# One weight unit of the compression moved to the room of the transposed queries, and the on-chip tiles at other addresses

## The chip, the cores and the metric

The kernel runs on one core of a Trainium2 chip. The metric is the device time of one launch in microseconds (us). The kernel before took 658.87 us, the median of three runs (658.71 to 659.05).

## The reference

Two layers of a decoder trunk on 256 tokens of width 1024, in float32. Each layer normalises its input, projects it once, feeds three groups of heads, projects their joined output back, and runs an MLP.

```
for l in range(DEPTH):                                  # DEPTH = 2, 256 tokens, width 1024
    h = rms_norm(x, ln1_gain[l])
    proj = h @ w_in[l]                                  # 1024 x 2866, cut into q, k, v, gates, ...
    o_nsa = nsa_mixer(...)                              # compressed, selected and window branches, 6 heads
    o_mla = mla_mixer(...)                              # low-rank attention, 5 heads
    o_ret = retention_mixer(...)                        # chunkwise retention, 5 heads
    x = x + concatenate([o_nsa, o_mla, o_ret]) @ w_out[l]
    h = rms_norm(x, ln2_gain[l])
    x = x + jnp.square(jax.nn.relu(h @ w_up[l])) @ w_down[l]        # 1024 -> 4096 -> 1024
return rms_norm(x, final_gain)
```

The change touches the first step of the compressed branch. Blocks of 32 keys and of 32 values, one starting every 16 tokens, get a position embedding and go through a two-layer network of their own:

```
blk = tok[:, tok_idx] + pos_emb[None, None, :, None, :]     # 15 blocks of 32 tokens
flat = blk.transpose(...).reshape(b, 15, g, 32 * 64)
return jax.nn.gelu(flat @ w1) @ w2                          # w1: 2048 x 128, one for keys, one for values
```

## The kernel before

**Engines.** TensorE (PE) multiplies, VectorE (DVE), ScalarE (ACT) and GpSimd (POOL) do the elementwise work, SyncE (SP) issues nearly all transfers. Each engine works through its instructions in a fixed order, and waits where the next one is not ready. That order is made when the program is built: the kernel's lines are issued with priorities (the table `PRIO`, the calls of `prio`), and a scheduler with a model of the durations sets the order of each engine from them. So where a tile gets its room later or earlier, the scheduler may order every engine anew.

**Products.** Each float32 operand is cut into a high part and a low part, both in a rounded 32-bit type. `mm3` (L151 to L153) makes one product of three matmuls. In the in-projection, in the out-projection and in the down projection the weights are the moving operand (384, 320, 434 or 512 columns at a time) and the activations are loaded into the array as stationary tiles of 128 x 128. In the up projection it is the other way round: weights stationary, the transposed activations `xT` moving, 512 columns with `hi_wu` (L1120) and 256 with `lo_wu` (L1121). There are 512 such pairs (the first 32 of them under the name `l_pu`).

**Weights.** They stream in units of 4 KB a partition, in the order of a list that the class `Stream` walks: for each layer `A`, the low-rank weights, `B2`, the small tables of the compression, `B1` (4 units, queries), `w1` (4 units: two for keys, two for values), `B3` (4 units), `rq`, `rk`, `rg`, `rv`, `wo`, then `wu` and `wd` of the MLP. A unit is loaded to a raw tile (`raw_tile`, pool `rawp`, five buffers, DMAs at L328), cut by a cast on ACT (L145, high part) and a subtraction on DVE (L146, low part) into tiles of the pool `splitp` (five buffers each), and used from there. A raw buffer comes free when both have read it. The `w1` units (L421) are not cut: the matmuls of `ps_h` (L775) read the raw tiles, so four of the five raw buffers stay occupied from their load until `ps_h` has run, and the units behind them, `B3_0` to `B3_3` and `rq_0`, pass one after another through the fifth.

**The stretch around the compression.** ACT scales a value tile (`l_vm`, L669), copies transposed queries and keys (`l_qkT`, L677), copies the transposed blocks `l_T` (L756, L758, L760) and the key tile `l_kT`, and cuts units of `B3` in between. When both halves of `l_T` are there, PE runs the 64 small matmuls of `ps_h` (L775). ACT copies the result to `h_sb` (L778), PE transposes and folds it into `ps_hT` (L781), and behind it on PE come the matmuls of `B3`. The chain from `ps_hT` over a gelu to `kc_` gives the compressed keys that the scores need later.

**Where the tiles lie.** Pools are laid out in the order in which they are opened. In the built program of the kernel before, all large tiles (raw, high and low parts of weights, `xs`, the scratch tiles, `xT`, the mixer's output, the probabilities and `u_h`, `u_l` of the MLP) start at 128 modulo 1024 bytes of a partition. `xT` (16 KB) lies in the pool `whole`; so do the transposed queries `qT0` and `qT1` (3 KB each), which are written for the first time after `ps_h` and last read by the scores of the same layer.

Of the kernel before, what the change touches and what calls it, by code (L numbers as in the profile page):

```python
# [7 lines left out]
F32 = mybir.dt.float32  # L8
F32R = mybir.dt.float32r
# [5 lines left out]
P = 128  # L15
D = 1024
S = 256
# [10 lines left out]
C_ID, C_INV, N_C0 = 0, 128, 176  # L28
# [49 lines left out]
def tile_hybrid_trunk(  # L78
# [25 lines left out]
):  # L104
    nc = tc.nc

    rawp = ctx.enter_context(tc.tile_pool(name="rawp", bufs=RAW))
    splitp = ctx.enter_context(tc.tile_pool(name="splitp", bufs=SPL))
    whole = ctx.enter_context(tc.tile_pool(name="whole", bufs=1))
    const = ctx.enter_context(tc.tile_pool(name="const", bufs=1))  # L110
    p1 = ctx.enter_context(tc.tile_pool(name="p1", bufs=1))
    p2 = ctx.enter_context(tc.tile_pool(name="p2", bufs=2))
# [3 lines left out]
    def prio(key):  # L116

        return tc.high_priority(offset=PRIO[key]) if key in PRIO else nullcontext()
# [7 lines left out]
    def wk(name, chain="N"):  # L126

        return wkp.tile([P, 512], F32, name=name, tag="wk" + chain)

    def scr(name, shape, dtype=F32, chain="N"):  # L130

        if chain == "N":
            return whole.tile(shape, dtype, name=name, tag="sN", bufs=5)
        return p2.tile(shape, dtype, name=name, tag="sM", bufs=7)
# [8 lines left out]
    def split(hi, lo, src, eng=nc.vector):  # L143

        a = nc.scalar.copy(out=hi, in_=src)  # L145
        b = eng.tensor_tensor(lo, src, hi.bitcast(F32), op=ALU.subtract)  # L146
        return a, b
# [9 lines left out]


    xs = whole.tile([P, 2, D], F32, name="xs")
    c0s = const.tile([P, N_C0], F32, name="c0s")  # L160
    c1s = const.tile([P, N_C1], F32, name="c1s")
    pos_i = const.tile([P, 2], I32, name="pos_i")
    xv = x.rearrange("o (t p) d -> p (o t) d", p=P)
# [21 lines left out]

    nc.gpsimd.dma_start(pos_i, positions.rearrange("o (t p) -> p (o t)", p=P))
    ident = c0s[:, C_ID:C_ID + P]
    gT = const.tile([P, 8], F32, name="gT")
    tri = c1s[:, C_TRI:C_TRI + 384]
    valid = c1s[:, C_VALID:C_VALID + 1]  # L190
    blk = c1s[:, C_BLK:C_BLK + 384]
# [123 lines left out]
    def raw_tile(name):  # L315
        return rawp.tile([P, 1024], F32, name="raw_" + name, tag="raw")
# [43 lines left out]
    def add_side(l, name, f):  # L360
        def load():
            side[l, name] = f()
        W.add((l, name), load)
# [37 lines left out]

    def add_cmp(l):
        def small():
            w2s = p1.tile([P, 3, 64], F32, name=f"l{l}_w2s", tag="w2s")
            pos_t = p1.tile([P, 2, 2, 64], F32, name=f"l{l}_pos_t", tag="pos_t")
            for z, (pe, w2) in enumerate(((cmp_pos_k, cmp_w2_k), (cmp_pos_v, cmp_w2_v))):
                nc.sync.dma_start(w2s[:, 2 * z], w2[l])
                for rep in range(8):
                    nc.sync.dma_start(pos_t[rep * 16:(rep + 1) * 16, z], pe[l].rearrange("(b a) d -> a b d", b=2))
            nc.sync.dma_start(w2s[:, 1], cmp_w2_k[l])  # L410
            return w2s, pos_t

        add_side(l, "cmp", small)

    def add_w1(l):
        for z, w1 in enumerate((cmp_w1_k, cmp_w1_v)):
            for i in range(2):
                def load(z=z, w1=w1, i=i):
                    raw = raw_tile(f"w1_{l}{z}{i}")
                    for b in range(2):  # L420
                        nc.sync.dma_start(  # L421
                            raw[b * 64:(b + 1) * 64].rearrange("p (a h) -> p a h", a=8),
                            w1[l, b * 1024 + i * 512:b * 1024 + (i + 1) * 512].rearrange("(a d) h -> d a h", d=64))
                    return raw
                W.add((l, "w1", z, i), load)
# [53 lines left out]
            add_down(l, c)  # L479


    xT2 = whole.tile([P, 8, 2, S], F32R, name="xT", tag="xT")
    xT = [xT2[:, :, i] for i in range(2)]

    class Line:
# [70 lines left out]
    for l in range(DEPTH):  # L556
        L = f"l{l}_"
# [171 lines left out]
        w2s, pos_t = side[l, "cmp"]  # L729
# [46 lines left out]
        with prio("cmp"):  # L776
            hs_ = scr("h_sb", [P, 256])
            nc.scalar.copy(out=hs_, in_=psh[:, 0:256])  # L778
            pst = wk("ps_hT")
            for z in range(2):  # L780
                nc.tensor.matmul(pst[:, z * 32:(z + 1) * 32], hs_[:, z * P:(z + 1) * P], fold, start=True, stop=True)  # L781
            hT = p2.tile([P, 64], F32, name="hT", tag="hT", bufs=1)
            g1 = p2.tile([P, 64], F32, name="g1", tag="g1", bufs=1)
            g2 = p2.tile([P, 64], F32, name="g2", tag="g2", bufs=1)
            nc.vector.tensor_copy(out=hT, in_=pst[:, 0:64])

            nc.vector.tensor_tensor(g1, hT, hT, op=ALU.mult)
            nc.vector.tensor_scalar(g1, g1, 0.044715, 1.0, op0=ALU.mult, op1=ALU.add)
            nc.vector.tensor_tensor(g1, g1, hT, op=ALU.mult)
            nc.scalar.activation(g2, g1, AF.Tanh, scale=0.7978845608028654)  # L790
            nc.vector.scalar_tensor_tensor(g1, in0=g2, scalar=1.0, in1=hT, op0=ALU.add, op1=ALU.mult)
            gv = p2.tile([P, 2, 3, 16], F32, name="gv", tag="gv", bufs=1)
            nc.gpsimd.tensor_copy(gv, g1[:, 32:64].rearrange("p (g n) -> p g n", g=2).unsqueeze(2)
                                  .broadcast_to([P, 2, 3, 16]))
            pc = wk("ps_kc")
            nc.tensor.matmul(pc[:, 0:32], w2s[:, 0:2].rearrange("p b d -> p (b d)"), g1[:, 0:32], start=True, stop=True)
            nc.tensor.matmul(pc[0:96, 64:128], gv.rearrange("p g r n -> p (g r n)"), w2s[:, 2], start=True, stop=True)
            kc_ = p2.tile([P, 32], F32, name="kc_", tag="kc_", bufs=1)
            nc.scalar.mul(kc_, pc[:, 0:32], 0.5)
            split(kT[0][:, :, 256:272], kT[1][:, :, 256:272], kc_.rearrange("p (g n) -> p g n", g=2))  # L800
            vcb = p2.tile([96, 3, 2, 64], F32, name="vcb", tag="vcb", bufs=1)
            nc.vector.tensor_tensor(vcb, blk[0:96].rearrange("p (r g d) -> p r g d", r=3, g=2),
                                    pc[0:96, 64:128].unsqueeze(1).unsqueeze(1).broadcast_to([96, 3, 2, 64]),
                                    op=ALU.mult)

        qT = [whole.tile([P, 3, S], F32R, name=f"{L}qT{g}", tag=f"qT{g}") for g in range(2)]
        kv_sb = [None, None]

        def evac_b1(t, ps):
# [511 lines left out]
```

## Time and profile before

| what | value |
|---|---|
| median of three runs | 658.87 us (658.71 to 659.05) |
| profiled execution | 659.2 us, of which its span 657.4 us |
| granted TensorE clock, mean over the span | 0.990 of 2.4 GHz |
| PE busy | 639.2 us, 97% of the span |
| DVE, ACT, POOL busy | 459.1 us (70%), 380.5 us (58%), 68.0 us (10%) |
| transferred | 111.64 MB, mean 170 GB/s |

The span runs from the first instruction to the last. A row of a timeline has the start, the duration, the engine, the line, the operation, output and inputs, the shape and how many instructions are joined; in square brackets is how long the engine stood idle before it and what ended that. The matmul rows overlap, since matmuls are pipelined: what one costs in a run of equals is the distance from start to start, not the duration.

### The profile page before, as it was taken

To read this page: it belongs to the slowest core of one execution; us is meant where nothing else is said; L and a number is where in the kernel's file an instruction comes from. 1 tells how busy PE (TensorE), PEld (TensorE's weight loads), DVE (VectorE), ACT (ScalarE), POOL (GpSimd) and SP (SyncE) were. 2 spreads that over 40 slices of the span, in tenths; PEclk is the share of its full clock that TensorE was granted. 3 is DMA by queue.
4 is the path that set the end of the run, shared out by engine and by line. 5 is a ranking of instruction groups with operands and counts; after the bars stand their busy time and mean duration, and the time that the engine had idled before them with its cause. 6 is when DMAs were issued, how large, how long until landed. Compare 5 with 4: busy or idle time off the path is not lost.

```text
span 657.4 us, 10417 instructions
## 1 busy us (share of the span) xinstructions
PE 639.2 (97%) x3619; PEld 549.4 (84%) x3619; DVE 459.1 (70%) x1063; ACT 380.5 (58%) x895; POOL 68.0 (10%) x124
## 2 busy tenths in 40 slices
PE   5999999999999999999999999999999999999995
PEld 4998998677888888888889999967688888888884
DVE  6666988767756666666685698887695666666663
ACT  5768786555546444444476887836364645444442
POOL 3320500300000000000023132120100000000000
PEclk7899999999999999999999999999999999999999
DMA  7877637152756565655538574532376465646521
GB/s 242 260 164 232 202 102 200 36 157 72 253 191 218 167 207 178 194 191 188 162 113 208 178 222 130 146 97 82 107 263 191 163 219 162 219 164 218 167 65 64
DMA packets 79796, 111.64 MB, mean 170 GB/s; under 512 B 9720, under 2 KB 67968, under 8 KB 79616
## 3 DMA queue, kind: packets, MB, share of 16 engines
q1 hardware_dynamic: 79136, 108.89, 53.9%
q0 software_dynamic: 608, 2.10, 1.0%
q8 instruction: 28, 0.46, 0.3%
q14 instruction: 24, 0.20, 0.1%
HBM read 109.92 MB, written 1.05 MB: 169 GB/s over the span
## 4 chain that ended last, share of the span: by engine, by line
PE 91%; DVE 3%; ACT 2%; DMA 1%; issue 1%; SPq 1%; POOL 0%; POOLq 0%; ACTq 0%
PE ps_up L1120 17%; PE l_pd L151 9%; PE l_pd L152 9%; PE l_pd L153 9%; PE ps_up L1121 9%; PE l_B L152 2%; PE l_B L153 2%; PE l_B L151 2%; PE l_oT L908 2%; PE l_po L151 2%; PE l_po L153 2%; PE l_po L152 2%; PE ps_pT L916 1%; PE l_pu L1120 1%; PE l_A L151 1%; PE ps_sm L694 1%
## 5 line engine op out<-in xcount | busy, mean ns | idle before, releaser
L1120 PE MATMUL ps_up<-xT,hi_wu 128*128 128x512 f32 x480 | 170.0, 398 | 0.0
L1121 PE MATMUL ps_up<-xT,lo_wu 128*128 128x256 f32 x480 | 133.6, 280 | 0.0
L146 DVE TENSOR_TENSOR lo_wd<-raw_wd,hi_wd 128x1024 fp32r<-128x1024 f32 x64 | 78.2, 1224 | 50.8 <-ACT hi_wd L145 50.4
L1120 PEld LDWEIGHTS ps_up<-xT,hi_wu 128*128 128x128 f32 x480 | 89.8, 188 | 21.4
L152 PE MATMUL l_pd<-lo_wd,u_h 128*128 128x512 f32 x256 | 99.9, 390 | 0.0
L151 PE MATMUL l_pd<-hi_wd,u_l 128*128 128x512 f32 x256 | 99.8, 391 | 0.0
L153 PE MATMUL l_pd<-hi_wd,u_h 128*128 128x512 f32 x256 | 99.6, 389 | 0.0
L145 ACT CAST hi_wu<-raw_wu 128x512 fp32r<-128x512 f32 x128 | 72.9, 618 | 40.8 <-issue 26.9
L146 DVE TENSOR_TENSOR lo_wu<-raw_wu,hi_wu 128x512 fp32r<-128x512 f32 x128 | 82.4, 685 | 18.2 <-ACT hi_wu L145 18.0
L1121 PEld LDWEIGHTS ps_up<-xT,lo_wu 128*128 128x128 f32 x480 | 90.6, 189 | 1.6
L145 ACT CAST hi_wd<-raw_wd 128x1024 fp32r<-128x1024 f32 x64 | 67.1, 1051 | 30.9 <-PE l_pd L153 20.5
L151 PEld LDWEIGHTS l_pd<-hi_wd,u_l 128*128 128x128 f32 x256 | 48.1, 188 | 10.4
L153 PEld LDWEIGHTS l_pd<-hi_wd,u_h 128*128 128x128 f32 x256 | 48.1, 188 | 10.2
L152 PEld LDWEIGHTS l_pd<-lo_wd,u_h 128*128 128x128 f32 x256 | 48.1, 188 | 8.8
L145 ACT CAST u_h<-u_u 128x512 fp32r<-128x512 f32 x32 | 19.8, 620 | 48.9 <-DVE u_u L1136 48.8
L1133 ACT COPY u_s<-ps_up 128x256 f32<-128x256 f32 x60 | 22.1, 369 | 40.1 <-PE ps_up L1121 40.1
L146 DVE TENSOR_TENSOR lo_B<-raw_B,hi_B 128x192 fp32r<-128x192 f32 (+1 forms) x80 | 28.7, 414 | 20.9 <-ACT hi_B L145 20.9
L1134 DVE TENSOR_TENSOR u_s<-ps_up,u_s 128x256 f32<-128x256 f32 x60 | 25.1, 420 | 25.9 <-ACT u_s L1133 25.9
L872 ACT ACTIVATE p_nsa<-p_nsa,nsa_m 128x256 f32<-128x256 f32 (+2 forms) x72 | 28.4, 397 | 11.0 <-DVE nsa_m L870 11.0
L146 DVE TENSOR_TENSOR u_l<-u_u,u_h 128x512 fp32r<-128x512 f32 x32 | 22.1, 690 | 16.8 <-ACT u_h L145 16.6
L152 PE MATMUL l_B<-lo_B,xT 128*128 128x384 f32 x96 | 32.9, 342 | 0.2 <-DVE lo_B L146 0.2
L151 PE MATMUL l_B<-hi_B,xT 128*128 128x384 f32 x96 | 32.8, 348 | 0.0
(325 smaller groups left out, 1266.2 us busy)
## 6 DMA issues: line engine op xcount, KB each, us to landing
raw_wu<-in_w_up_dram SPq DMA_DIRECT2D x64, 512.0 KB, 4.5
raw_wd<-in_w_down_dram SPq DMA_DIRECT2D x64, 512.0 KB, 4.2
raw_B<-in_w_in_dram SPq DMA_DIRECT2D x24, 384.0 KB, 3.6
raw_wo<-in_w_out_dram SPq DMA_DIRECT2D x10, 512.0 KB, 3.5
raw_A<-in_w_in_dram SPq DMA_DIRECT2D x8, 434.0 KB, 4.5
raw_wo<-in_w_out_dram SPq DMA_DIRECT2D x12, 256.0 KB, 4.1
raw_w<-in_cmp_w_k_dram SPq DMA_DIRECT2D x8, 256.0 KB, 4.1
raw_w<-in_cmp_w_v_dram SPq DMA_DIRECT2D x8, 256.0 KB, 3.9
```

The lines of the kernel that those rows point to most:

```text
L145: a = nc.scalar.copy(out=hi, in_=src)
L146: b = eng.tensor_tensor(lo, src, hi.bitcast(F32), op=ALU.subtract)
L151: nc.tensor.matmul(o, a[1], b[0], start=start, stop=False)
L152: nc.tensor.matmul(o, a[0], b[1], start=False, stop=False)
L153: return nc.tensor.matmul(o, a[0], b[0], start=False, stop=stop)
L694: nc.tensor.matmul(ps[:, i * 256:i * 256 + nk], qkT[:, 5 + h, t * P:(t + 1) * P], qkT[:, h, 0:nk], start=True, stop=True)
L872: nc.scalar.activation(p[:, o:o + n], p[:, o:o + n], AF.Exp, scale=-1.0, bias=ms[:, r, b:b + 1], accum_out=ls[:, r, b:b + 1])
L908: nc.tensor.matmul(oT[gp, 0:384], kv_sb[kt][:, vi, gp], pTs[g][:, 0:384], start=i == 0, stop=False)
L1120: nc.tensor.matmul(ps[j], w[0][:, o:o + P], x2, start=i == 0 and k == 0, stop=False)
L1121: last = nc.tensor.matmul(ps[j][:, 0:S], w[1][:, o:o + P], x2[:, 0:S], start=False, stop=i == 1 and k == 3)
L1133: nc.scalar.copy(sj, ps[j][:, S:512])
L1134: nc.vector.tensor_tensor(sj, ps[j][:, 0:S], sj, op=ALU.add)
```

## The change

Two things change. First, of the four `w1` units of a layer the first (keys, first half) goes to a tile of the pool `whole` with the tag `qT`, whose room serves the transposed queries later; `qT0` and `qT1` become one tile of 6 KB for that. So the unit needs no raw buffer, and only three of five are held until `ps_h`. Second, four tiles move to new pools (`front`, `between`, `actp`), which are opened before and after the big ones. In the built program that puts the raw, high and low weight tiles, `xs`, the scratch, the mixer's output, `u_h` and `u_l`, and the `qT` tile at 576 modulo 1024 bytes, and `xT` at 992. No arithmetic changes.

```diff
+    front = ctx.enter_context(tc.tile_pool(name="front", bufs=1))
     rawp = ctx.enter_context(tc.tile_pool(name="rawp", bufs=RAW))
     splitp = ctx.enter_context(tc.tile_pool(name="splitp", bufs=SPL))
     whole = ctx.enter_context(tc.tile_pool(name="whole", bufs=1))
+    between = ctx.enter_context(tc.tile_pool(name="between", bufs=1))
+    actp = ctx.enter_context(tc.tile_pool(name="actp", bufs=1))
     const = ctx.enter_context(tc.tile_pool(name="const", bufs=1))
...
-    c0s = const.tile([P, N_C0], F32, name="c0s")
+    c0s = front.tile([P, N_C0], F32, name="c0s")
...
-    gT = const.tile([P, 8], F32, name="gT")
+    gT = between.tile([P, 8], F32, name="gT")
...
-            w2s = p1.tile([P, 3, 64], F32, name=f"l{l}_w2s", tag="w2s")
+            w2s = front.tile([P, 3, 64], F32, name=f"l{l}_w2s", tag="w2s")
...
                 def load(z=z, w1=w1, i=i):
-                    raw = raw_tile(f"w1_{l}{z}{i}")
+                    raw = raw_tile(f"w1_{l}{z}{i}") if z or i else whole.tile([P, 1024], F32, name=f"l{l}_w1a", tag="qT")
...
-    xT2 = whole.tile([P, 8, 2, S], F32R, name="xT", tag="xT")
+    xT2 = actp.tile([P, 8, 2, S], F32R, name="xT", tag="xT")
...
-            gv = p2.tile([P, 2, 3, 16], F32, name="gv", tag="gv", bufs=1)
+            gv = between.tile([P, 2, 3, 16], F32, name="gv", tag="gv", bufs=1)
...
-        qT = [whole.tile([P, 3, S], F32R, name=f"{L}qT{g}", tag=f"qT{g}") for g in range(2)]
+        qT2 = whole.tile([P, 2, 3, S], F32R, name=L + "qT", tag="qT")
+        qT = [qT2[:, g] for g in range(2)]
```

The scheduler answers with another order on every engine. On SP, in layer 1, this is what stood around the `w1` units before (a unit's name has the layer, the chunk and the number; `w1_101` is layer 1, keys, second half):

```order
L421 DMA raw_w1_100_3780<-in_cmp_w1_k_dram 64x8x128 x2
L421 DMA raw_w1_101_3795<-in_cmp_w1_k_dram 64x8x128 x2
L421 DMA raw_w1_110_3798<-in_cmp_w1_v_dram 64x8x128 x2
L421 DMA raw_w1_111_4058<-in_cmp_w1_v_dram 64x8x128 x2
L328 DMA raw_1_B3_0_4101<-in_w_in_dram 128x2x384
L328 DMA raw_1_B3_1_4103<-in_w_in_dram 128x2x384
L328 DMA raw_1_B3_2_4105<-in_w_in_dram 128x2x384
L328 DMA raw_1_B3_3_4107<-in_w_in_dram 128x2x384
L328 DMA raw_1_rq_0_4214<-in_w_in_dram 128x3x320
```

The four loads of `w1` stand in a row there. Now it is:

```order
L426 DMA raw_w1_101_3803<-in_cmp_w1_k_dram 64x8x128 x2
L426 DMA raw_w1_110_3806<-in_cmp_w1_v_dram 64x8x128 x2
L426 DMA raw_w1_111_4066<-in_cmp_w1_v_dram 64x8x128 x2
L332 DMA raw_1_B3_0_4109<-in_w_in_dram 128x2x384
L332 DMA raw_1_B3_1_4111<-in_w_in_dram 128x2x384
L332 DMA raw_1_B3_2_4113<-in_w_in_dram 128x2x384
L332 DMA raw_1_B3_3_4115<-in_w_in_dram 128x2x384
L332 DMA raw_1_rq_0_4222<-in_w_in_dram 128x3x320
L332 DMA raw_1_rq_1_4234<-in_w_in_dram 128x3x320
```

The load of `w1_100` is gone from this place: as `l1_w1a` it is issued far ahead, in the MLP of layer 0 (in layer 0 right behind the constants `c1s`). With two raw buffers to pass through, each `B3` unit and `rq_0` no longer waits for the cut of the unit in front of it but for the one two in front.

On ACT, in layer 1, these are the instructions from the key tile to the copy of `h_sb` before, with the cut of one `B3` unit:

```order
L145 CAST l1_kT0_4109<-ps_ksT_4183 128x2x128
L677 COPY l1_qkT_3807<-ps_qkT_3918 96x4x128
L677 COPY l1_qkT_3807<-ps_qkT_3924 96x2x128
L756 COPY l1_T_4111<-ps_T_4199 64x4x128
L760 COPY l1_T_4111<-ps_T_4199 64x4x128
L145 CAST hi_1_B3_1_4244<-raw_1_B3_1_4103 128x192 x4
L677 COPY l1_qkT_3807<-ps_qkT_3928 96x4x128
L145 CAST l1_kT0_4109<-ps_ksT_4208 128x2x128
L677 COPY l1_qkT_3807<-ps_qkT_3934 96x4x128
L778 COPY h_sb_4302<-ps_h_4213 128x256
L607 ACTIVATE q_sb_4379<-l1_B10_4329,l1_rstd_3678 128x2x3x64
```

Only one `B3` unit is cut in this piece. Now it is:

```order
L149 CAST l1_kT0_4117<-ps_ksT_4191 128x2x128
L149 CAST hi_1_B3_2_4272<-raw_1_B3_2_4113 128x192 x4
L682 COPY l1_qkT_3815<-ps_qkT_3926 96x4x128
L682 COPY l1_qkT_3815<-ps_qkT_3932 96x2x128
L761 COPY l1_T_4119<-ps_T_4207 64x4x128
L765 COPY l1_T_4119<-ps_T_4207 64x4x128
L149 CAST l1_kT0_4117<-ps_ksT_4216 128x2x128
L149 CAST hi_1_B3_3_4292<-raw_1_B3_3_4115 128x192 x4
L682 COPY l1_qkT_3815<-ps_qkT_3936 96x4x128
L682 COPY l1_qkT_3815<-ps_qkT_3942 96x4x128
L149 CAST hi_1_rq_0_4438<-raw_1_rq_0_4222 128x960
L783 COPY h_sb_4310<-ps_h_4221 128x256
```

The cut of `B3_0` now stands ahead of the value tile `l1_vm1` and that of `B3_1` ahead of this piece, which begins with the key tile; the cuts of `B3_2` and `B3_3` and the cast of `rq_0`, which stood behind `h_sb`, now stand in front of it. Layer 0 moves in the same way. On PE the matmuls of `ps_h`, `ps_hT` and `B3` keep their order in both layers, with `ps_hT` ahead of all `B3` matmuls.

## Rows read from the trace of the kernel before

**Rows 1.** The page: busy time and instructions of each engine
```profile
PE 639.2 (97%) x3619; PEld 549.4 (84%) x3619; DVE 459.1 (70%) x1063; ACT 380.5 (58%) x895; POOL 68.0 (10%) x124
```
**Rows 2.** Waits of PE: waited for, total us, times, longest
```profile
PE l_A L151 <- DVE xT L146: 4.5, 1, 4.5
...
PE ps_pT L916 <- ACT pT L920: 0.8, 2, 0.4
PE ps_s L855 <- DVE nsa_m L870: 0.6, 2, 0.3
...
PE ps_qkT L676 <- ACT l_qkT L677: 0.5, 1, 0.5
PE ps_sm L694 <- ACT l_qkT L677: 0.3, 1, 0.3
```
**Rows 3.** Timeline of ACT in layer 1, from the value tile to h_sb
```profile
362.58 0.53 ACT L669 ACTIVATE l_vm<-ps_uv,rsm 128x320 f32<-128x320 f32 x1 [0.44 <-PE ps_uv L153]
...
364.65 1.12 ACT L145 CAST hi_B<-raw_B 128x192 fp32r<-128x192 f32 x4
367.22 0.37 ACT L145 CAST l_kT<-ps_ksT 128x256 fp32r<-128x256 f32 x1 [1.45 <-PE ps_ksT L737]
...
369.52 1.11 ACT L145 CAST hi_B<-raw_B 128x192 fp32r<-128x192 f32 x4
...
372.16 0.37 ACT L778 COPY h_sb<-ps_h 128x256 f32<-128x256 f32 x1 [0.16 <-ACT l_qkT L677]
...
378.14 0.98 ACT L145 CAST hi_rq<-raw_rq 128x960 fp32r<-128x960 f32 x1
```
**Rows 4.** Timeline of SP and of PE in layer 1, same stretch
```profile
366.23 0.37 SPq L328 DMA_DIRECT2D raw_B<-in_w_in_dram  x1
...
369.97 1.99 PE L775 MATMUL ps_h<-raw_w,l_T 128*32 128x128 f32 x64
...
373.02 0.53 PE L781 MATMUL ps_hT<-c1s,h_sb 128*128 128x32 f32 x4
```
**Rows 5.** Tile raw_B, 350 to 378 us: issue to landing
```profile
DMA to landing us min/median/max: 3.2/3.4/3.9
```
**Rows 6.** Timeline of ACT in layer 0, the same piece
```profile
44.75 0.53 ACT L669 ACTIVATE l_vm<-ps_uv,rsm 128x320 f32<-128x320 f32 x1 [0.42 <-PE ps_uv L153]
...
49.36 0.37 ACT L145 CAST l_kT<-ps_ksT 128x256 fp32r<-128x256 f32 x1 [1.43 <-PE ps_ksT L737]
...
52.81 1.13 ACT L145 CAST hi_B<-raw_B 128x192 fp32r<-128x192 f32 x4 [1.25 <-DMA raw_B<-in_w_in_dram]
...
55.18 0.39 ACT L778 COPY h_sb<-ps_h 128x256 f32<-128x256 f32 x1
```
**Rows 7.** Timeline of PE in layer 0, the same piece
```profile
52.11 1.99 PE L775 MATMUL ps_h<-raw_w,l_T 128*32 128x128 f32 x64
...
56.32 0.53 PE L781 MATMUL ps_hT<-c1s,h_sb 128*128 128x32 f32 x4
```
**Rows 8.** Timeline of PE in an up projection: ten pairs
```profile
480.64 0.40 PE L1120 MATMUL ps_up<-xT,hi_wu 128*128 128x512 f32 x1
...
483.82 0.40 PE L1120 MATMUL ps_up<-xT,hi_wu 128*128 128x512 f32 x1
```
**Rows 9.** Timeline of PE in a down projection
```profile
491.66 0.39 PE L152 MATMUL l_pd<-lo_wd,u_h 128*128 128x512 f32 x1
...
499.82 0.39 PE L152 MATMUL l_pd<-lo_wd,u_h 128*128 128x512 f32 x1
```
**Rows 10.** Timeline of PE in chunk rq of layer 1
```profile
389.14 0.31 PE L151 MATMUL l_rq<-hi_rq,xT 128*128 128x320 f32 x1
...
390.61 0.31 PE L152 MATMUL l_rq<-lo_rq,xT 128*128 128x320 f32 x1
```
**Rows 11.** Groups of PE by form: instructions of the up projection
```profile
L1120 PE MATMUL ps_up<-xT,hi_wu 128*128 128x512 f32 x480 | 170.0, 398 | 0.0
...
L1120 PE MATMUL l_pu<-xT,hi_wu 128*128 128x512 f32 x32 | 12.1, 414 | 0.6 <-DVE xT L536 0.6
```
**Rows 12.** Tile l_qT: casts on ACT, first and last start
```profile
L825 ACT CAST l_qT<-ps_qT x4: 463/463/473, 68.8 to 392.7; 128x384 fp32r<-128x384 f32 x4
```
**Rows 13.** Windows: us, busy of each engine, clock, DMA share, GB/s
```profile
56.32:155.10 98.78, 97.33 (x613) 82.67 (x611) 80.29 (x276) 63.87 (x202) 18.62 (x29) 1.00 0.49 147
...
373.02:471.79 98.77, 97.30 (x613) 82.65 (x611) 80.46 (x276) 64.07 (x203) 18.73 (x29) 1.00 0.48 145
```

## The prediction

> **What bounds the kernel now.** I read the page's first part, then what PE waits for, then the stretch that the change touches on ACT, SP and PE, and last the distances between matmuls. The page has PE busy for 97% of the span [rows 1]: it is the bound, and only two things can move the time, an idle stretch of PE or another price for one of its matmuls. The list of PE's waits shows how little idle time there is to win [rows 2]: 4.5 us for `xT` in front of the first matmuls of `A`, which this change doesn't touch, and then waits below 1 us each. Four of these belong to the attention: 0.5 us for a copy of `l_qkT`, 0.3 us for another one in front of the scores `ps_sm`, and 0.8 and 0.6 us (both layers together) in front of `ps_pT` and `ps_s`. Behind `ps_hT` PE runs on a fixed load: from its start to the first up matmul 98.78 us pass in layer 0 and 98.77 in layer 1, with PE busy for 97.3 in either [rows 13]. So what delays `ps_hT` by a microsecond delays the end by up to one, unless those later waits take it up.
>
> **The freed raw buffer and the order of ACT, layer 1.** The unit `w1a` needs no buffer, so `B3_2`, `B3_3` and `rq_0` are loaded one cut earlier, and the order puts their casts in front of `h_sb`. Before, ACT goes from the value tile at 362.58 to the end of `h_sb` at 372.16 + 0.37 = 372.53, and stands idle within it for 1.45 and 0.16 us [rows 3]. Now two cuts of 1.11 us and the cast of `rq_0` of 0.98 us come into this piece [rows 3]: 3.20 us of added work on ACT, less 1.61 us of idle time, so at least 1.6 us later if nothing else moves. The cut of `B3_0` (1.12 us) only changes places with the value tile. Some 0.4 us of this PE hides itself: before, `ps_hT` starts at 373.02, 0.49 us after `h_sb` ends, because PE is still in `ps_sm` [rows 3, 4].
>
> Step by step: the cut of `B3_0` starts about 362.6, and `B3_2` may be loaded when DVE has subtracted, which took 366.23 − 364.65 = 1.6 us before [rows 3, 4]: 364.2, landed 3.4 us later [rows 5] at 367.6. Its cast follows the key tile (367.22 + 0.37), ends at 368.7, and pushes the second half of `l_T` back, and with it `ps_h`, by 0.8 to 1.1 us from 369.97 [rows 4]. `B3_3` is loaded when `B3_1` is cut (about 366.9, landed 370.3), and `rq_0` when `B3_2` is cut (about 369.2, landed 372.6 to 373.1, the slowest landing being 3.9). From the later `l_T` on ACT has the key tile, a cut of 1.11, two copies and the cast of 0.98: it ends near 374.1, and `h_sb` 0.37 later at 374.4 to 374.7. `ps_hT` comes at 374.4 to 374.7 in place of 373.02: 1.4 to 1.7 us later. I take +1.4. PE has nothing to put in between, as the matmuls of `B3` stand behind `ps_hT` in its order. Bounds: 0 if the cast of `rq_0` finds its data early and all else is overlapped; +2.1 if both `B3_3` and `rq_0` land at the slowest 3.9.
>
> **The same in layer 0.** The idle time of ACT is larger there, 1.43 and 1.25 us [rows 6], and the second of these, a wait for a transfer of `B3_1`, goes, since `B3_1` is now loaded two units earlier. From the value tile at 44.75 to the end of `h_sb` at 55.18 + 0.39 = 55.57 are 10.82 us, 8.14 of them work; with 3.20 more it is 11.34, so 56.1 at best, and 57.1 if the wait for the key tile stays at half a microsecond and one transfer is late by as much. `ps_hT` was at 56.32 [rows 7]: 0 to +0.8, and I take +0.4. That the removed wait is worth something shows from `ps_h` to `ps_hT`: 4.21 us in layer 0, 3.05 in layer 1 [rows 4, 7], so 1.16 us is the most that can be won here, and it is the bound below.
>
> **What is given back.** The casts moved ahead are missing later, so ACT is ahead in front of the first scores, where PE waited 0.8 + 0.6 us [rows 2]. Of these 1.4 us I take 0.4; the bounds are 0 and 1.4.
>
> **The room of the queries.** `w1a` shares its tile with the queries. Their first cast starts at 68.8 us [rows 12], 16 us after `ps_h` (52.11), and in layer 1 the unit's load can start when layer 0's scores have run, long before it is wanted. No wait, 0. SP issues the unit far ahead, in layer 0 behind `c1s` and ahead of `B1_0`, where its two DMAs at 0.37 us each [rows 4] hold `B1_0` back by 0.7 us; PE had no wait for a `B1` unit among the larger ones [rows 2]. I take 0, with 0 and +0.7 as bounds.
>
> **The addresses.** This is the unknown, because in the trace of before all large tiles start at 128 modulo 1024. What can be read is how far a start within a tile matters. In chunk `rq` the moving weights begin at columns 0, 320 and 640 of their tile, at three different offsets modulo 1024 bytes, and ten matmuls take 390.61 − 389.14 = 1.47 us, evenly 147 ns, for 320 columns, which at 2.4 GHz are 133.3 ns [rows 10]. So each matmul costs 13.5 ns over its columns, whatever its offset. In the down projection 36 steps take 8.16 us, 226.7 ns for 512 columns (213.3), again 13.4 ns over [rows 9]. Only the up pair is dearer: nine pairs in 483.82 − 480.64 = 3.18 us are 353.3 ns a pair, 33.3 ns over its 768 columns (320.0) where two matmuls at 13.4 would have 26.8 [rows 8]. If the 6.5 ns hang on the addresses of the weights against those of `xT`, then 480 + 32 pairs [rows 11] are worth 512 x 6.5 ns = 3.3 us. Since no offset that the trace shows changes a distance, I take 0, with −3.3 and, for the same size the other way, +3.3 as bounds.
>
> [...]
>
> **Sum.** 1.4 + 0.4 − 0.4 + 0 + 0 = +1.4 us. The profiled execution took 659.2 us (span 657.4 and 1.8 outside it), 0.3 over the median; on the median the sum gives 658.9 + 1.4 = **660.3 us**.
>
> **The rivals.**
>
> *A, slack takes it.* The transfers land early, PE's waits at `ps_qkT` and `ps_sm` (0.5 + 0.3) go, and the 1.4 us in front of the later scores are all given back. Then 1.8 − 1.4 − 0.8 = −0.4: about 658.5. For it: the order in layer 0 has 2.7 us of idle time on ACT. Against: ACT in layer 1 has half of what it needs.
>
> *B, the up pairs get cheaper* with weights and `xT` at different residues, down to the down projection's price: 1.4 − 3.3 = −1.9, **657.0 us**. For it: the up pairs alone pay more, and only they move `xT` past the weights. Against: the offsets inside the tiles show nothing. It decides if a pair falls below 350.6 ns, where 512 pairs give back the 1.4 us.
>
> *C, the early loads win*, with `ps_hT` on time in layer 1 because PE is busy enough in front of it: −1.2 (layer 0) − 1.4 (later waits) = −2.6, 656.3 us. Against: `h_sb` stands behind the cast of `rq_0`.
>
> *D, the up pairs get dearer* by the same 6.5 ns: +1.4 + 3.3 = 663.6 us.
>
> **How the numbers follow.** What a measurement of this kernel can tell from no change is about 0.2%, 1.3 us: below 657.6 is faster, above 660.2 slower. The forecast has 0.40; its own range is 659.5 to 661.4 (from 1.4 + 0 with 0.8 given back to 1.7 + 0.8 with nothing given back), of which five eighths lie above 660.2: 0.25 slower, 0.15 same. A has 0.16, all same. B 0.22: 0.20 faster, 0.02 same. C 0.13: 0.12 faster, 0.01 same. D 0.09, slower. Together faster 0.32, same 0.34, slower 0.34. The range reaches down over C and most of B, where early loads and cheaper pairs may add up, to 655.2, and up over the forecast and the smaller half of D, to 662.8.
>
> **What would show it.** In the profile after: `ps_hT` at 374.4 or later on the clock of before in layer 1 (right), or at 373.0 (A or C); the wait of PE for `h_sb` as a new line of some 1 us each among PE's waits; the waits for `l_qkT` gone; nine up pairs in 3.18 us (right), 3.12 (B) or 3.24 (D); 226.7 and 147 ns kept in the down projection and in `rq`. The prediction is wrong if the distances of matmuls in any chunk change by over 1%, since 2% of PE's time is more than everything else here.

## The result, and the profile after

The changed kernel is slower: 666.5 us (median of four runs, 664.8 to 668.7) against 659.0 us of the kernel before beside it, a ratio of 1.0101 with a 95% interval of 1.0077 to 1.0125. The forecast was 660.3 us, its range 655.2 to 662.8. The profiled execution took 668.65 us with a span of 666.9 us, and is the slowest of the four, so what follows accounts for +9.5 us of span where the medians differ by 7.5, and 2 us of it are more than the median lost.

First the stages, as windows of the kernel after, cut at the starts of `ps_hT`, of the first up matmul and of the first matmul of `l_A` (columns as in [rows 13]):

```profile
63.70:163.80 100.10, 97.06 (x612) 82.61 (x610) 76.26 (x267) 61.16 (x194) 18.65 (x29) 1.00 0.47 137
382.35:482.63 100.28, 97.25 (x612) 82.81 (x612) 77.07 (x268) 61.61 (x195) 18.69 (x29) 1.00 0.43 130
163.80:341.61 177.81, 177.79 (x909) 151.49 (x909) 120.35 (x177) 93.12 (x163) 0.63 (x1) 1.00 0.61 191
482.63:666.90 184.27, 177.06 (x900) 150.66 (x900) 119.10 (x174) 92.06 (x160) 2.20 (x3) 0.99 0.53 172
341.61:382.35 40.74, 39.55 (x283) 36.95 (x283) 27.31 (x74) 31.34 (x88) 11.42 (x27) 1.00 0.61 155
```

The windows of the kernel before that [rows 13] do not hold:

```profile
155.10:334.36 179.26, 179.26 (x909) 151.66 (x909) 120.30 (x177) 93.16 (x163) 0.63 (x1) 1.00 0.60 189
471.79:657.40 185.61, 178.47 (x900) 150.77 (x900) 118.99 (x174) 92.11 (x160) 2.20 (x3) 0.99 0.52 170
334.36:373.02 38.66, 38.66 (x283) 37.05 (x283) 24.68 (x65) 28.96 (x80) 11.33 (x27) 1.00 0.56 144
```

| stretch | before | after | difference |
|---|---|---|---|
| start to `ps_hT`, layer 0 | 56.32 | 63.70 | +7.4 |
| `ps_hT` to the first up matmul, layer 0 | 98.78 | 100.10 | +1.3 |
| MLP of layer 0, to the first `l_A` of layer 1 | 179.26 | 177.81 | −1.45 |
| first `l_A` to `ps_hT`, layer 1 | 38.66 | 40.74 | +2.1 |
| `ps_hT` to the first up matmul, layer 1 | 98.77 | 100.28 | +1.5 |
| MLP of layer 1 and the end | 185.61 | 184.27 | −1.34 |

So most of the loss lies in the first 64 us, some in the rest of the attention, and the MLPs won. The waits of PE in the kernel after, beside those of [rows 2]:

```profile
PE l_po L155 <- DVE l_mixT L150: 3.3, 2, 1.6
...
PE ps_uv L155 <- ACT qf L666: 1.7, 1, 1.7
PE ps_qkT L681 <- ACT l_qkT L682: 1.7, 2, 0.9
PE ps_ksT L742 <- DVE l_kT L150: 1.4, 1, 1.4
PE l_rg L155 <- ACT l_rk L612: 1.4, 2, 0.7
...
PE l_B L155 <- ACT l_kc L612: 0.9, 1, 0.9
```

The waits at `ps_s` and `ps_pT` are gone, as the forecast had it, and new ones stand at places that it did not name. The wait for `l_qkT`, which was to go, grew from 0.5 to 1.7 us, and the forecast wait of PE for `h_sb` is not there. ACT in layer 0, the kernel after, the same piece as [rows 6] and a little ahead of it:

```profile
37.21 1.11 ACT L149 CAST hi_B<-raw_B 128x192 fp32r<-128x192 f32 x4 [5.22 <-PE l_B L157]
...
50.48 1.11 ACT L149 CAST hi_B<-raw_B 128x192 fp32r<-128x192 f32 x4 [3.68 <-DMA raw_B<-in_w_in_dram]
51.50 0.52 ACT L674 ACTIVATE l_vm<-ps_uv,rsm 128x320 f32<-128x320 f32 x1
...
61.26 1.00 ACT L149 CAST hi_rq<-raw_rq 128x960 fp32r<-128x960 f32 x1 [0.43 <-DMA raw_rq<-in_w_in_dram]
62.77 0.37 ACT L783 COPY h_sb<-ps_h 128x256 f32<-128x256 f32 x1 [0.51 <-PE ps_h L780]
```

Two casts wait. The one at 37.21 is the first cut of `B1_0`: the profile names PE, but this unit was issued at 25.17 and the tile's slowest landing in that stretch is 12.0 us, so it landed at 37.2. Landings of `raw_B`, 24 to 42 us, before and after:

```profile
DMA to landing us min/median/max: 5.0/7.3/7.3
...
DMA to landing us min/median/max: 7.5/7.6/12.0
```

The cast at 50.48 is the cut of `B3_0`, which now stands ahead of the value tile. ACT waits 3.68 us for its transfer, and the value tile and the copies of `l_qkT` and `l_T`, whose inputs had been ready, wait behind it; PE then waits for these copies. The clock falls in that stretch, as the windows of the kernel after show (PE busy first, the granted clock third from the end):

```profile
52.00:54.00 2.00, 1.61 (x13) 1.27 (x12) 0.78 (x3) 1.96 (x6) 0.42 (x1) 1.00 0.30 45
54.00:56.00 2.00, 0.57 (x4) 0.29 (x2) 1.58 (x6) 1.48 (x6) 0.00 (x0) 0.91 0.51 172
56.00:58.00 2.00, 1.12 (x6) 0.79 (x5) 1.08 (x4) 1.99 (x7) 0.00 (x0) 0.50 0.75 205
58.00:60.00 2.00, 2.00 (x26) 1.55 (x28) 1.11 (x4) 1.98 (x7) 0.00 (x0) 0.50 0.82 221
60.00:62.00 2.00, 2.00 (x44) 1.85 (x40) 0.39 (x2) 1.57 (x3) 0.00 (x0) 0.50 0.20 53
```

PE was busy for 0.57 of 2 us, and from 56 to 62 us it was granted a clock of 0.50 of full speed; before, it stayed at 1.00 from 40 to 64 us. `ps_h`, 1.99 us before [rows 7], runs within that and takes 3.6:

```profile
59.05 1.09 PE L780 MATMUL ps_h<-l_w1a,l_T 128*32 128x128 f32 x16
59.91 2.73 PE L780 MATMUL ps_h<-raw_w,l_T 128*32 128x128 f32 x48
```

So the 7.4 us that layer 0 loses up to `ps_hT` are made up like this. From the last matmul of `l_A` (25.39) to the first of `ps_qkT` (47.02) it loses 3.2, from there to `ps_h` (59.05) 4.5, and from `ps_h` to `ps_hT` 0.4; 0.8 us come back ahead of that, because the clock rose from 0.50 to 1.00 earlier within `l_A` in this execution (at 18.1 us in place of 20.1; from 18 to 20 us PE started 12 matmuls, and 7 before). The fallen clock is hardly in the 4.5 us, since `ps_h` starts 0.59 us after ACT's last copy of `l_T` ends, and 0.56 before. It shows in the idle 0.51 us in front of `h_sb` above.

ACT in layer 1, the kernel after:

```profile
370.00 1.11 ACT L149 CAST hi_B<-raw_B 128x192 fp32r<-128x192 f32 x4 [0.44 <-PE ps_uv L157]
...
375.80 1.11 ACT L149 CAST hi_B<-raw_B 128x192 fp32r<-128x192 f32 x4 [0.63 <-DMA raw_B<-in_w_in_dram]
...
381.03 0.99 ACT L149 CAST hi_rq<-raw_rq 128x960 fp32r<-128x960 f32 x1
381.93 0.36 ACT L783 COPY h_sb<-ps_h 128x256 f32<-128x256 f32 x1
```

Here the cut of `B3_0` (370.00) waits no longer than the value tile did in that place before, 0.44 us [rows 3]. The cut of `B3_2` waits 0.63 us for its transfer, and `h_sb` stands directly behind the cast of `rq_0`.

Last the up pairs, after, nine of them in 3.13 us, 347.8 ns each, against 353.3 [rows 8]:

```profile
491.12 0.39 PE L1126 MATMUL ps_up<-xT,hi_wu 128*128 128x512 f32 x1
...
494.25 0.39 PE L1126 MATMUL ps_up<-xT,hi_wu 128*128 128x512 f32 x1
```

512 pairs by 5.5 ns are 2.8 us, which is what the two MLP stretches won.

### The profile page after: what moved, and what is told of

Its sections match the earlier page's. It is cut to its first block, busy times and chain, and to the rows that moved or that the text cites. A ratio compares the mean times of both kernels' runs of the same rounds, so it can differ in the third digit from the quotient of the medians.

```text
span 666.9 us, 10417 instructions
## 1 busy us (share of the span) xinstructions
PE 639.9 (96%) x3619; PEld 550.4 (83%) x3619; DVE 457.6 (69%) x1063; ACT 380.3 (57%) x895; POOL 68.2 (10%) x124
## 4 chain that ended last, share of the span: by engine, by line
PE 84%; DVE 6%; ACT 5%; DMA 2%; issue 1%; SPq 1%; POOL 0%; POOLq 0%; ACTq 0%; DVEq 0%
PE ps_up L1126 17%; PE l_pd L157 9%; PE l_pd L155 9%; PE l_pd L156 9%; PE ps_up L1127 8%; PE l_po L155 2%; PE l_oT L914 2%; PE l_po L157 2%; PE l_po L156 2%; PE l_B L156 2%; PE l_B L157 2%; PE l_B L155 2%; DVE lo_rg L150 2%; DMA raw_B<-in_w_in_dram 1%; PE ps_pT L922 1%
## 5 line engine op out<-in xcount | busy, mean ns | idle before, releaser
L1126 PE MATMUL ps_up<-xT,hi_wu 128*128 128x512 f32 x480 | 167.6, 392 | 0.0
L150 DVE TENSOR_TENSOR lo_wd<-raw_wd,hi_wd 128x1024 fp32r<-128x1024 f32 x64 | 78.2, 1225 | 50.3 <-ACT hi_wd L149 49.9
L149 ACT CAST hi_B<-raw_B 128x192 fp32r<-128x192 f32 (+1 forms) x80 | 25.2, 381 | 18.7 <-PE l_B L157 7.4
```

The lines of the kernel that those rows point to most:

```text
L1126: nc.tensor.matmul(ps[j], w[0][:, o:o + P], x2, start=i == 0 and k == 0, stop=False)
```

## The experiments

The times of one group of runs are compared with the kernel before on the same chip (659.3 to 659.5 us). The theory at the outset: w1a's early load costs layer 0, ACT's order costs something in both layers, the addresses win.

**The addresses alone.** The first `w1` unit goes back to a raw buffer in both layers.

```diff
-  raw = raw_tile(f"w1_{l}{z}{i}") if z or i else whole.tile([P, 1024], F32, name=f"l{l}_w1a", tag="qT")
+  raw = raw_tile(f"w1_{l}{z}{i}")
```

> The changed kernel with the first w1 unit back in a raw buffer in both layers: the new addresses alone, in the order of before. Theory 1 (the loss comes from the early load of w1a and from ACT's order, the addresses only win): the up pairs keep 347 ns in place of 353.3, 512 pairs win 2.9 us, so about 656.0 us, 0.995 of before. Rival (the addresses also cost the attention something, in transposes, ACT or DVE): 659 us or more, with longer durations or distances outside the MLP.

657.2 us, ratio 0.9964 (0.9952 to 0.9976): faster. The up pairs are at the pace of the kernel after, and from `ps_hT` to the first up matmul of layer 0 pass 99.02 us (98.78 before), so the attention pays 0.2 us a layer for the addresses, no more. The order on PE, ACT and DVE is that of before. A part of the price shows in the matmuls of `l_B`: 19 of them take 3.36 us in the kernel after (48.07 to 51.43), 176.8 ns each, and 17 take 2.95 before (45.60 to 48.55), 173.5 ns each.

**The room alone**, the kernel before with that line and the merged `qT` tile, all at 128:

> The kernel before with only the w1 unit moved to the room of the queries, all tiles still at 128 modulo 1024. Theory 1: the up pairs stay at 353.3 ns and the whole loss is there: 666.5 + 2.9 = 669.4 us. Rival (addresses cost the attention): 659 to 662 us, since most of the loss goes with the old addresses.

670.0 us, ratio 1.0155 (1.0133 to 1.0176). The whole loss is here, 10.8 us in place of 7.5, since the addresses' gain is missing. The order on PE, ACT, DVE and POOL is the changed kernel's.

**The room in layer 1 only** (`if z or i or l == 0 else`):

> The changed kernel with the first w1 unit in a raw buffer in layer 0 and in the room of the queries in layer 1. Theory 1: layer 0's loss of some 8.7 us up to its first up matmul goes, layer 1 keeps its own (2.0 us up to ps_hT and 1.5 us behind it), the addresses win 2.9: 658.9 + 3.5 - 2.9 = 659.5 us. Rival (the loss is the same mechanism in both layers, ACT's order, and layer 1's is small only by chance of the state): half of it stays, 662 us or more.

661.1 us, ratio 1.0026 (1.0013 to 1.0040), nearer to the rival's number in the median. By stages the theory holds: layer 0 is as before up to `ps_hT` (56.78), and layer 1 takes 374.31 − 333.56 = 40.75 us from `l_A` to `ps_hT`, the changed kernel's 40.74, and 100.29 behind it. Layer 1's loss of 3.6 us is its own, with half of the new waits of PE:

```profile
PE l_po L155 <- DVE l_mixT L150: 1.7, 1, 1.7
...
PE l_rg L155 <- ACT l_rk L612: 0.7, 1, 0.7
```

**w1a behind B1 in layer 0.**

```diff
+  last_load[0] = nc.sync.dma_start(view(raw), src)      # at every load of a unit
...
+  with tc.issue_after(last_load[0].ins) if not (l or z or i) else nullcontext():   # the load of B1_3
       nc.sync.dma_start(raw[b * 64:(b + 1) * 64]..., w1[l, ...])
```

> The changed kernel with one dependence more: in layer 0 the loads of w1a are issued behind the load of the last B1 unit, where the first w1 unit stood before; the room, the addresses and the early loads of B3 stay. Theory 1 (layer 0 loses because 0.5 MB of w1a stand ahead of B1 in the queue while the transfers are the bound): ps_h of layer 0 starts near 53 us in place of 59, the time is 659.5 + 1 to 3 for layer 0's ACT order = 660.5 to 662.5 us. Rival (layer 0 loses by ACT's order alone): ps_h at 58 or later and 665 us or more.

666.9 us, ratio 1.0107 (1.0087 to 1.0128): the rival was right about the time. The first wait went: `ps_qkT` of layer 0 starts 0.5 us later than before, not 2.5 (0.1 and 3.2 counted from the last matmul of `l_A`). But `ps_h` is still 5.2 us late, and the median is no lower than the changed kernel's 666.5. The order on PE, ACT, DVE and POOL is the changed kernel's, so only the place of these loads differs. ACT in this kernel, layer 0:

```profile
33.26 1.11 ACT L149 CAST hi_B<-raw_B 128x192 fp32r<-128x192 f32 x4
...
48.68 1.11 ACT L149 CAST hi_B<-raw_B 128x192 fp32r<-128x192 f32 x4 [3.86 <-DMA raw_B<-in_w_in_dram]
49.70 0.52 ACT L676 ACTIVATE l_vm<-ps_uv,rsm 128x320 f32<-128x320 f32 x1
```

The cut of `B1_0` no longer waits, the cut of `B3_0` does. SP issued its transfer at 41.50, and it landed at 48.6. The kernel before issued the same load later and cut it earlier, without a wait (its timelines of SP and ACT):

```profile
43.35 0.37 SPq L328 DMA_DIRECT2D raw_B<-in_w_in_dram  x1
...
46.81 1.11 ACT L145 CAST hi_B<-raw_B 128x192 fp32r<-128x192 f32 x4
```

With one more buffer to pass through, the last `w1` units (one of their loads was issued at 40.44) and `B3_1` were in flight together with it. So the theory was changed: what costs is the place that the scheduler gave to the cuts.

**The cut of B3_0 behind `l_T` again**, in both layers, nothing else edited:

```diff
+  behind = after_.get(self.done)          # for B3_0: the second copy of l_T's first half
-  with prio("split"):
+  with prio("split"), tc.issue_after(behind.ins) if behind else nullcontext():
       u[3] = u[1](u[2])
...
+  last = nc.scalar.copy(out=T[64:128, :, :, 0:112], in_=pv[64:128, :, :, 16:P])
...
+  if t in CUTS:                           # CUTS = (0,)
+      after_[W.index[l, "B3", t]] = last
```

> The changed kernel with one dependence more in each layer: the cut of B3_0 on ACT comes behind the first two copies of l_T, as before, in place of ahead of the value tile; w1a keeps its room and its early load. Theory 2, from the run with w1a behind B1 (layer 0 loses because ACT, which works in order, waits some 3.8 us for B3_0's transfer in front of the value tile and the copies of l_qkT and l_T): that wait goes, ps_h of layer 0 starts at 55 us or before in place of 59, and the time is 662 to 663 us. Rival (the early loads crowd the transfers, and everything that waits for a unit is late wherever it stands): 665 us or more.

665.5 us, ratio 1.0083 (1.0059 to 1.0107). Neither number: the time is the rival's, the place of the loss the theory's. Between `ps_qkT` and `ps_h` layer 0 loses 0.7 us (4.5 in the changed kernel), since the value tile no longer waits behind the cut. The unit lands as late as in the changed kernel, near 50.3, and costs little where it now stands:

```profile
46.73 0.53 ACT L677 ACTIVATE l_vm<-ps_uv,rsm 128x320 f32<-128x320 f32 x1 [0.42 <-PE ps_uv L158]
...
50.29 2.20 ACT L150 CAST hi_B<-raw_B 128x192 fp32r<-128x192 f32 x8 [1.52 <-DMA raw_B<-in_w_in_dram]
```

In layer 1, where only the two cuts stand ahead of `h_sb` and not the cast of `rq_0`, `l_A` to `ps_hT` takes 39.84 us: +1.2 in place of +2.1. But one dependence made the scheduler order all the rest anew, and behind `ps_hT` 3.0 us are lost in layer 0 where the changed kernel loses 1.3.

**All four cuts in their places of before**, with `W.hold` and `W.release` around `h_sb` and the dependence above for `B3_0` and `B3_1`:

> The changed kernel with the four cuts of B3 held in the places on ACT that they had before: B3_0 behind the first half of l_T, B3_1 behind the second, B3_2 and B3_3 behind h_sb. The room, the early loads and the addresses stay. Theory 2: with the order of before the whole loss goes, also layer 1's (ps_hT on time, no waits at l_rg and l_po), and what is left is the addresses' gain and up to 2 us for w1a's early load in layer 0: 657 to 659 us. Rival (the early loads cost by themselves): 661 us or more.

668.4 us, ratio 1.0131 (1.0111 to 1.0151): the theory's 657 to 659 us missed, and the rival's number came, though not by its mechanism: up to `ps_hT` the theory held. `ps_hT` of layer 0 starts at 54.67, 1.65 us earlier than before, and layer 1 takes 38.80 us to it (38.66). So with the old places the early loads win up to `ps_hT`: 1.17 of the 1.65 us lie between `ps_h` and `ps_hT` (3.04 us in place of 4.21), which is the bound that the prediction had for the removed wait. The rest, 0.5 us, lies within `l_A`. Behind `ps_hT` yet another order came out, which loses 7.2 and 6.0 us (waits of 3.7 us a layer for the retention's norm, and behind each the clock is granted at 0.50, for 6.8 and 3.4 us; its mean over the span is 0.983, and 0.990 before). A dependence put in by hand that changes the order on other engines is no clean test of a total here; the stretch is.

**A buffer held.** w1a keeps its room and its early load, but an empty tile takes the freed buffer until `h_sb` is there:

```diff
+  if not (z or i):                            # in front of the load of the first w1 unit
+      held[l] = raw_tile(f"held_{l}")
+      nc.gpsimd.memset(held[l][:, 0:8], 0.0)
...
+  nc.gpsimd.tensor_tensor(gT, held[l][:, 0:8], hs_[:, 0:8], op=ALU.add)     # behind the copy of h_sb
```

> The changed kernel, with w1a in the room of the queries and loaded early, but with the fifth raw buffer held by an empty tile from the place of the first w1 unit until h_sb is there, so that B3 passes through one buffer as before; the order on ACT is that of before again. Theory 3 (the loss comes from the orders that the scheduler makes of the freed buffer, not from the room and the early load): ps_hT and all behind it as with the addresses alone, 657.2 us, plus 0 to 3 us where w1a delays B1: 657 to 660 us. Rival (the early load of w1a costs by itself, as a transfer): 662 us or more.

657.5 us, ratio 0.9960 (0.9940 to 0.9979): the loss is gone. On PE and ACT the order is that of before up to `ps_hT` of layer 0 and in the whole of layer 1; in the rest of layer 0's attention it is yet another, which costs nothing. From `ps_hT` to the first up matmul, both layers:

```profile
59.19:157.37 98.18, 96.94 (x612) 82.68 (x610) 80.19 (x276) 63.35 (x202) 19.86 (x29) 1.00 0.53 156
374.04:473.03 98.99, 97.55 (x613) 82.85 (x611) 80.56 (x276) 64.03 (x203) 18.50 (x29) 1.00 0.48 146
```

Only w1a ahead of `B1` still shows, as ACT's wait for `B1_0` in layer 0:

```profile
37.62 1.11 ACT L149 CAST hi_B<-raw_B 128x192 fp32r<-128x192 f32 x4 [5.30 <-DMA raw_B<-in_w_in_dram]
```

From the last matmul of `l_A` to `ps_qkT` it cost 3.2 us in this execution, the slowest of its ten, and in that of the changed kernel, 1.6 with the room alone, 1.7 with `B3_0`'s cut moved, 0.1 with all cuts moved: it differs from one profiled execution to the next. The medians do not show it: 657.5 us here and 657.2 with the addresses alone, 666.5 in the changed kernel and 666.9 with w1a behind `B1`, and the intervals of the ratios overlap in both pairs.

**Both places in layer 0 at once:**

> The changed kernel with both dependences: w1a of layer 0 loaded behind B1, and the cut of B3_0 behind the first half of l_T. Read by the stretch up to ps_h of layer 0: theory 3 (w1a ahead of B1 costs 0 to 3 us in front of ps_qkT, the cut of B3_0 ahead of the value tile some 4 us between ps_qkT and ps_h, and the two add up) has ps_qkT within 0.5 us and ps_h within 1.5 us of before, and some 663.5 us in all, 2 less than with the cut alone moved, the rest being lost behind ps_hT as there. Rival (one of them merely moves the other's wait): ps_h 3 us late or more.

664.8 us, ratio 1.0075 (1.0050 to 1.0100). `ps_qkT` is 0.2 us late, `ps_h` 2.0, where 1.5 had been expected at most: the two add up roughly, with 1.8 us left between them. Even behind `l_T` the cut of `B3_0` waits for its transfer, and the cut of `B3_1` stands behind it, ahead of the key tile:

```profile
49.63 2.20 ACT L150 CAST hi_B<-raw_B 128x192 fp32r<-128x192 f32 x8 [2.62 <-DMA raw_B<-in_w_in_dram]
```

The order on PE, ACT, DVE and POOL is that of the run with the cut alone moved. Beside its ratio (1.0083, 1.0059 to 1.0107) w1a's place makes no difference here either that the medians can tell.

**Where xT lies.** The kernel before with `xT` in a pool of its own behind a pad of 416, 512 or 32 bytes, and the addresses of the changed kernel with another 608:

```diff
+  padp = ctx.enter_context(tc.tile_pool(name="padp", bufs=1))      # behind `whole`
+  actp = ctx.enter_context(tc.tile_pool(name="actp", bufs=1))
...
+  pad = padp.tile([P, PAD], F32, name="pad")       # PAD = 104, 128 or 8 words; 152 for all at 576
...
-  xT2 = whole.tile([P, 8, 2, S], F32R, name="xT", tag="xT")
+  xT2 = actp.tile([P, 8, 2, S], F32R, name="xT", tag="xT")
```

> The kernel before with xT alone at other addresses: 544 modulo 1024, weights and all else in the partition's first 140 KB still at 128, so xT starts 416 bytes behind the weights as in the changed kernel. The order is that of before. Theory R (the residue of xT against the weights decides): up pairs at 347 ns, 512 x 6 ns = 3 us less, 656 us. Rival A (the weights' own start decides, 576 in place of 128): 353.3 ns, 658.9 us.

> The addresses of the changed kernel without w1a's room, but with xT moved by another 608 bytes, so that weights and xT both start at 576 modulo 1024. Theory R (the residue of xT against the weights decides): up pairs back at 353 ns and 658.9 us. Rival A (the weights' own start decides): 347 ns and 656 to 657 us.

> The kernel before with xT alone moved, to 640 modulo 1024, 512 bytes behind the weights. Theory R1 (only equal residues modulo 1024 cost): up pairs at 347 ns, 656.7 us. Rival R2 (equal residues modulo 512 cost): 353 ns, 659 us.

> The kernel before with xT alone moved, to 160 modulo 1024, 32 bytes behind the weights. Theory R1 (any distance of 32 bytes will do): up pairs at 347 ns, 656.7 us. Rival R3 (weights and xT have to be some hundred bytes apart): pairs near 353 ns, 658 to 659 us.

| weights, `xT` modulo 1024 | distance | up pair | time, ratio (interval) |
|---|---|---|---|
| 128, 128 (before) | 0 | 353.3 ns | 659 us |
| 128, 544 | 416 | 347.8 ns | 656.7, 0.9959 (0.9940 to 0.9977) |
| 576, 576 | 0 | 353.3 ns | 661.4, 1.0028 (1.0013 to 1.0043) |
| 128, 640 | 512 | 353.3 ns | 659.5, 1.0011 (0.9993 to 1.0029) |
| 128, 160 | 32 | 347.8 ns | 656.9, 0.9961 (0.9946 to 0.9977) |

In these rows the distance decides, not the weights' own start: theory R, by the second and third row. A distance of 512 cost as much as one of 0, 353.3 ns, which is R2; other distances were not tried, 256 among them. The pairs at a distance of 512 bytes, nine in 3.18 us:

```profile
480.51 0.40 PE L1125 MATMUL ps_up<-xT,hi_wu 128*128 128x512 f32 x1
...
483.69 0.64 PE L1125 MATMUL ps_up<-xT,hi_wu 128*128 128x512 f32 x2
```

And at 32 bytes, nine in 3.13:

```profile
480.25 0.39 PE L1125 MATMUL ps_up<-xT,hi_wu 128*128 128x512 f32 x1
...
483.38 0.40 PE L1125 MATMUL ps_up<-xT,hi_wu 128*128 128x512 f32 x1
```

That all at 576 took 2 us more than before with the same pairs is another matter. In its profiled execution the wait for `l_qkT` behind `ps_h` was 1.43 us (0.50 before [rows 2]), and then the clock fell in a stretch where it had stayed at 1.00:

```profile
54.00:56.00 2.00, 0.42 (x2) 0.17 (x2) 1.48 (x5) 1.98 (x7) 0.00 (x0) 1.00 0.30 38
56.00:58.00 2.00, 1.97 (x8) 1.73 (x8) 0.84 (x4) 1.37 (x5) 0.00 (x0) 0.64 1.00 351
58.00:60.00 2.00, 2.00 (x8) 2.00 (x8) 2.00 (x12) 1.49 (x6) 0.00 (x0) 0.50 0.88 284
60.00:62.00 2.00, 2.00 (x8) 2.00 (x7) 1.13 (x6) 2.00 (x9) 0.00 (x0) 0.50 1.07 370
62.00:64.00 2.00, 2.00 (x7) 1.69 (x7) 0.19 (x1) 1.20 (x2) 0.00 (x0) 0.65 1.02 306
```

The matmuls of `B3` at a clock of 0.50 cost it 3 us between `ps_hT` and `l_rg`. But this execution took 663.3 us, and only one other of the ten has its mean clock of 0.984; why the median of 661.4 is above the kernel before stays open.

Four runs beat both kernels and are not told apart: `xT` 416 or 32 bytes on (656.7 and 656.9 us), the addresses alone (657.2) and the buffer held (657.5).

## Why the prediction was wrong

The direction was right, the size wrong by a factor of five, because the forecast took layer 0 for a copy of layer 1 with more slack. The addresses' 2.8 us, which it took at nothing, even hid a part of the miss: with the room alone it is 10.8 us.

- *"The cut of `B3_0` only changes places with the value tile."* This is the step that failed. It is true in layer 1, where the unit has landed. In layer 0 ACT waits 3.7 us for the transfer, and everything behind the cast on ACT waits with it (the value tile starts at 51.50, directly behind the cast): 4.5 us between `ps_qkT` and `ps_h`. The step was made with ACT's idle time as a pool into which work can be put; that idle time was of no use to a cast that itself waited 3.68 us for its transfer. The run with that cut moved back shows it (0.7 us left, though the unit lands as late), that with w1a behind `B1` shows that it isn't w1a's transfer (4.8 us stay, in the same order). Layer 0's term was +0.4, and it measured +7.4 in the profiled execution.
- *"Its two DMAs hold `B1_0` back by 0.7 us."* The issue was priced and not the transfer. w1a's half megabyte is issued behind `c1s` and ahead of `B1`, and the slowest landing of `raw_B` went from 7.3 us in the same stretch before to 12.0. It cost 3.2 us in the profiled execution, 0.1 to 3.2 over the profiled executions of five kernels. In the medians no cost of it can be told, so the 0 that the sum took for it is not shown to be wrong.
- *Layer 1, +1.4.* The mechanism was right and the size near: +2.1, the upper bound. The terms (two cuts, one cast ahead of `h_sb`) hold: without the cast of `rq_0` +1.2 is left, with none of them +0.1. What was too small is the time until the cut of `B3_2`: its load is issued at 372.50, which is 365.25 on the clock of before (less 7.25 us), where the forecast had 364.2.
- *"What is given back", −0.4.* The two waits went as forecast, but the order behind `ps_hT` loses 1.3 and 1.5 us in their place (`l_rg` and `l_po`). That it comes with the freed buffer's order shows from the buffer held, −0.6 and +0.2, clearest in layer 1, where the order is that of before; which instruction of the changed order does it was not tried.
- *The addresses, 0.* Rival B was right in sign, cause and size: 353.3 to 347.8 ns, 2.8 us won of the 3.3 that the sum bounded. By the prediction's own sign (a distance that changes by over 1%) that alone made it wrong. The reason given against it was not sound: the offsets in chunk `rq` vary the moving weights against `xT` as the stationary operand, which is not the case in which the pairs lose. Nine pairs at their quickest in these runs take 347.8 ns each. The 2.4 columns a ns by which the prediction took the columns' share of a matmul can be read from its own rows: 147 ns for 320 columns and 226.7 for 512 are 79.7 ns for 192 more [rows 9, 10].

A range that took in a late transfer at the head of ACT's queue in layer 0 would have held the result. No rival had it.

## What to carry to other kernels

A buffer that comes free lets the scheduler move casts forward, and here a cast that waited 3.68 us for its transfer held up all that stood behind it on ACT: for each instruction that moves ahead, ask when its data lands in that stage, above all in the first stage, where `raw_B` took 3.3 to 6.6 us from issue to landing here (43 to 53 us; 3.1 to 4.5 in layer 1, 358 to 386 us). Price a load that moves by its bytes ahead of others, not by its issue: with w1a's half megabyte ahead, the slowest landing of `raw_B` was 12.0 us in place of 7.3, where 0.7 us had been allowed for the issue. Look at the start addresses of a matmul's two operands too: here a pad of 32 bytes won almost as much in the two MLPs as 416 did (2.4 us and 2.8), without the dearer matmuls of `l_B`.

## What the runs showed of the hardware that was not expected

- An fp32r matmul pair with 512 and 256 moving columns took 353.3 ns where the tiles of the moving operand and of the stationary weights start 0 or 512 bytes apart modulo 1024, and 347.8 ns at 32 and 416. The matmuls of `l_B` (384 columns, `xT` stationary) go the other way, from 174 to 176 ns at 416 and not at 32 (medians of their distances in layer 1). The down projection stayed at 227 ns for 512 columns, before and after, with all at 576 and with `xT` 512 or 32 bytes on; both its operands start at equal residues modulo 1024.
- A stall of PE in layer 0 was followed by a lower clock in one run and not in another: with all at 576, PE waited 1.43 us behind `ps_h` and was then granted 0.50 for some 7 us (56.6 to 63.4). With the addresses alone the wait was 1.3 us at the same place, and the clock stayed at 1.00 (50 to 64 us).
- With w1a behind `B1`, `B3_0` was issued 1.85 us earlier than in the kernel before (41.50 against 43.35) and landed some 2 us later (at 48.6, against 46.5), with more transfers in flight beside it.
